# A hybrid backbone layer on one core: the later operands of seven products stored in two parts

## The chip, the core and the metric

The kernel runs on one core of a Trainium2 chip. The time is that of one execution on the device, in microseconds (us). The engines are TensorE (PE, matmuls; PEld is its weight loading), VectorE (DVE), ScalarE (ACT), GpSimd (POOL) and SyncE (SP, which here issues DMAs). All data are float32.

## What is computed

One layer for 1024 latent tokens and 256 context tokens of width 1024. A modulated, normalised input is projected by one wide matrix; then come windowed attention, a short gated convolution, a gated merge and an output projection, and a mixture of 16 experts. What matters here is the middle:

```
p = h @ w_in                        # columns: q, k, v | u, B, C | two gates
o = windowed attention of q, k, v   # 16 heads of 64, blocks of 128 queries
y = B * conv3(C * u)                # depthwise, width 3
merged = sigmoid(g_attn) * (o @ w_proj_attn) + sigmoid(g_conv) * (y @ w_proj_conv)
out = merged @ w_out
```

## The kernel before

TensorE multiplies float32 in parts: a number is stored as hi (its cast to the short format FR) and lo (what the cast left out, also as FR), and three matmuls, hi by hi, hi by lo and lo by hi, make a product. So an operand has to be split first: a ScalarE cast makes hi, a subtract on VectorE or GpSimd makes lo.

The program runs in stages. Attention (255 to about 597 us) goes through 32 units (class Unit), each of four heads by 128 queries; their matmuls and those of the two gate projections, 16 blocks of 48 (gate_half), stand between each other in an order that a scheduler made for ACT, DVE, PE and SP. What is left of the gate blocks is computed up to 624.9. At the end of a unit, ACT copies one half of its output from PSUM and DVE adds the other half; the result `ot`, 64 by 512, is stored to `od` in DRAM. On GpSimd a hand-written list of work (pool_work) runs beside it; its last items are o_sums(0) and o_sums(1), which load rows of `od` into tiles `acc` and `w` and make four sums of them.

The stage of the seven products (624.9 to 1054.6) computes the columns C, u, B of `p` and both projections. It is a loop over 20 pairs, each 128 columns of a weight and the same 128 columns 512 further on (class Pair). A pair is computed as a 2x2 block product in seven products instead of eight, one for each slot 0 to 6; a product is a call of block(), 12 matmuls of 128x512. The left operands are made from the weights (sums13, split22, sums24, split11, whose splits are the rows of L855 and L856). The right operands, four sums t1 to t4 and three plain blocks b11, b22, b21, are one set for pairs 0 to 11 (from the layer's input), a second set for pairs 12 to 15 (from `od`) and a third for pairs 16 to 19 (from the conv output `yd`). All three lie in the same SBUF buffers. In the order of slots 0 to 6 a pair takes t1, t3, b11, b22, t4, t2, b21. Normal pairs alternate between two groups of PSUM banks (names w, psT, psB, psF).

All engines run this stage in an order that is written by hand: the loop calls cur.product(slot), then the work of the slot, and then what at_turn(n, slot, f) has put there. For the second and third set, op_load(which, j) at turn (11 or 15, j + 1) loads the slot's operand, 1 MB, into its lo buffer, when the last pair of the old set has used it; op_split three turns later casts it to hi (L1005) and subtracts hi from it (L1006), half on DVE and half on POOL:

```
parts = ((nc.vector, slice(0, 2)), (nc.gpsimd, slice(2, 4)))
if which == 0 and j < 2:
    parts = ((nc.gpsimd, slice(0, 4)),)
```

The sums for t1 to t4 come from `sums[0]` and `sums[1]` in DRAM: of `od` by o_sums on POOL and, for the last two of four row blocks, by DVE in pairs 2 to 5 (o_late); of `yd` by DVE in pair 3m + 4 (sums_of). Weights come in by SP (L870), two tiles for each pair, one pair ahead.

Of the kernel before, what the change touches and what calls it, by code (L numbers as in the profile page):

```python
# [27 lines left out]
def hybrid_layer(ctx, tc, x, c, cx, c_ctx, w_mod, b_mod, norm1_g, w_in, attn_sink, conv_w,  # L28
# [60 lines left out]
    yd = dram.tile([NK, 128, T], F32, name="yd")  # L89
    sums = [dram.tile([4, NK // 2, 128, 512], F32, name=f"sums{i}") for i in range(2)]  # L90
# [370 lines left out]
    def mod_row(n, w_tile, acc_tile, more=False):  # L461


        def load(k):
            row, k = n + 2 + k // NK, k % NK
            w = w_tile()
            nc.gpsimd.dma_start(out=w, in_=w_mod[k * 128:(k + 1) * 128, row * 1024:row * 1024 + 1024])
            rws.append(w)

        if not rws:  # L470
            load(0)
            load(1)
            yield
        acc = acc_tile()
        for k in range(NK):
            w = rws.pop(0)
            nc.gpsimd.tensor_scalar(w if k else acc, w, sf[:, 0, k:k + 1], 1.0, op0=OP.mult, op1=OP.mult)
            if k:
                nc.gpsimd.tensor_tensor(out=acc, in0=w, in1=acc, op=OP.add)
            if k == NK - 1:  # L480
                nc.gpsimd.dma_start(out=rowp[n], in_=acc)
            if k < NK - 2 or more:
                load(k + 2)
            yield
# [122 lines left out]
    class Unit:  # L607
# [64 lines left out]
        def values(self, ci):  # L672
            if ci == 0:
                self.po = psB()
            th, tl = self.th.pop(ci)
            last = len(self.chunks) - 1
            nc.tensor.matmul(self.po, lhsT=self.v2t[:, self.chunks[ci]], rhs=th, start=(ci == 0), stop=False)
            nc.tensor.matmul(self.po, lhsT=self.v2t[:, self.chunks[ci]], rhs=tl, start=False, stop=(ci == last))  # L678
            if ci == last:
                g, i, po = self.g, self.i, self.po  # L680
                ot = at.tile([64, 512], F32, name="ot", bufs=3)
                nc.scalar.copy(out=ot, in_=po[64:128])
                nc.vector.tensor_tensor(out=ot, in0=po[0:64], in1=ot, op=OP.add)
                nc.sync.dma_start(out=od[g * 256:(g + 1) * 256, i * 128:(i + 1) * 128].rearrange("(h d) q -> d h q", h=4),
                                  in_=ot.rearrange("d (h q) -> d h q", h=4))
# [30 lines left out]
    def sums_of(eng, which, ks, p11, p12, p21, p22):  # L716

        for o_, a, b in ((p11, p12, p11), (p12, p22, p12), (p22, p22, p11), (p21, p21, p22)):
            eng.tensor_tensor(out=o_, in0=a, in1=b, op=OP.subtract)

    def sums_out(which, ks, p11, p12, p21, p22):
        for n, p in enumerate((p11, p12, p22, p21)):
            nc.sync.dma_start(out=sums[which][n, ks], in_=p)

    def o_rows(ks, p1, p2, eng=nc.sync):
        eng.dma_start(out=p1, in_=od[ks * 128:(ks + 1) * 128])
        for th in range(2):
            eng.dma_start(out=p2[th], in_=od[512 + ks * 128:512 + (ks + 1) * 128, th * 512:th * 512 + 512])
        return 0, ks, p1[:, 0:512], p1[:, 512:1024], *p2
# [7 lines left out]
    def pool_work():  # L737
        for n in range(1, 4):
            yield from mod_row(n, w_tile, lambda: osp.tile([128, 1024], F32, name="acc", bufs=2), n < 3)
        for ks in range(4):  # L740
            yield from x_sums(ks)
        for ks in range(2):

            yield from o_sums(ks)

    def o_sums(ks):
        o1, o2 = (osp.tile([128, 2, 512], F32, name=nm, bufs=2) for nm in ("acc", "w"))
        o = o_rows(ks, o1.rearrange("p a b -> p (a b)"), [o2[:, 0], o2[:, 1]], nc.gpsimd)
# [113 lines left out]
    class Pair:  # L862
# [39 lines left out]
        def quad(self, q):  # L902
# [33 lines left out]
            self.y_out(q)  # L936

        def y_out(self, q):
            if self.kind == 2 and q > 1:
                i = 3 - q  # L940
                nc.sync.dma_start(out=yd[self.m + 4 * i], in_=st["y"][i])
                if q == 3:
                    st["ys"] = (1, self.m, *[st["y"][a][:, b] for a in range(2) for b in (h0, h1)])
# [29 lines left out]
    def o_late(ks):  # L973
        st["o"] = o_rows(ks, mp_slot(7), [stage.tile([128, 512], F32, name="gs", bufs=2) for th in range(2)])
# [7 lines left out]
    def op_load(which, j):  # L982

        nm, at_ = takes[j]
        if nm[0] == "t":
            hi, lo = (tx.tile([128, 4, 512], FR, name=f"{nm}{hl}") for hl in range(2))
            src = sums[which][("t1", "t3", "t2", "t4").index(nm)].rearrange("k p f -> p k f")
        else:
# [3 lines left out]
            if which:  # L992
                src = yd[kh * 4:kh * 4 + 4, :, ts].rearrange("k p f -> p k f")
            else:
                src = od[kh * 512:kh * 512 + 512, ts].rearrange("(k p) f -> p k f", p=128)
        nc.sync.dma_start(out=lo.bitcast(F32), in_=src)
        opsets[which + 1][nm] = [hi, lo]

    def op_split(which, j):
        hi, lo = opsets[which + 1][takes[j][0]]  # L1000
        parts = ((nc.vector, slice(0, 2)), (nc.gpsimd, slice(2, 4)))
        if which == 0 and j < 2:
            parts = ((nc.gpsimd, slice(0, 4)),)
        for eng, ks in parts:
            nc.scalar.copy(out=hi[:, ks], in_=lo[:, ks].bitcast(F32))  # L1005
            eng.tensor_tensor(out=lo[:, ks], in0=lo[:, ks].bitcast(F32), in1=hi[:, ks].bitcast(F32), op=OP.subtract)  # L1006

    st, prev, later = {}, None, []

    def late_mults():  # L1010
        for q, o_, p in later:
            nc.gpsimd.tensor_tensor(out=o_, in0=p, in1=o_, op=OP.mult)
        prev.y_out(2)
        prev.y_out(3)
# [7 lines left out]
    for which, n in ((0, 12), (1, 16)):  # L1022
        for j in range(7):
            at_turn(n - 1, j + 1, lambda which=which, j=j: op_load(which, j))
            at_turn(n - 1, j + (5 if (which, j) == (0, 2) else 4), lambda which=which, j=j: op_split(which, j))
    for m in range(4):
        at_turn(3 * m + 4, 2, lambda: sums_of(nc.vector, *st["ys"]))
        at_turn(3 * m + 4, 5, lambda: sums_out(*st["ys"]))

    def row_load(n):  # L1030
        acc, small = mp_slot(4), mp_slot(5)
        br, nr = small[0:2, 0:512], small[0:2, 512:1024]
# [23 lines left out]
    for ks, b in ((2, 17), (3, 38)):  # L1056
        at_turn(0, b - 5, lambda ks=ks: o_late(ks))
        at_turn(0, b, lambda: sums_of(nc.vector, *st["o"]))
        at_turn(0, b + 3, lambda: sums_out(*st["o"]))
    at_turn(12, 5, late_mults)  # L1060
# [838 lines left out]
```

## Time and profile before

| | us |
|---|---|
| median of 3 runs | 1806.25 |
| lowest and highest | 1803.19 and 1810.12 |
| the profiled execution | 1805.46 |
| its span on the core | 1803.7 |

The profile is of one execution. Over the whole span TensorE is busy 1717.8 us (95%), VectorE 1418.4, ScalarE 1004.7 and GpSimd 553.5. The stage of the seven products takes 429.7 us of the span, attention about 342. Times of the trace are counted from the span's start. PEclk is the granted TensorE clock as a share of full speed; "idle before" is the time that an engine waited, and the arrow names what ended the wait.

### The profile page before, as it was taken

The page shows a single profiled execution, that of the slowest core. Times are in us where ns is not written, and L with a number is a line of the kernel's source. Part 1 is how long each engine was busy: PE and PEld are TensorE (multiplying, and loading weights), DVE is VectorE, ACT ScalarE, POOL GpSimd, SP SyncE. Part 2 cuts the span into 40 slices and gives each one's busy share as a digit, 9 for nine tenths or more (in the row PEclk, how much of TensorE's full clock was granted, in tenths as well). Part 3 has the DMA queues.
Part 4 walks back from the last instruction along what each step waited for, and adds up shares of the span by engine and source line. Part 5 has one row for each costly group of instructions (what it writes and reads, how often), then busy time and mean ns, then how long its engine had stood idle before and what let it go on. Part 6 is the DMA issues. An engine that isn't in the chain of part 4 may idle for free.

```text
span 1803.7 us, 24231 instructions
## 1 busy us (share of the span) xinstructions
PE 1717.8 (95%) x8421; PEld 1381.7 (77%) x8421; DVE 1418.4 (79%) x2018; ACT 1004.7 (56%) x1446; POOL 553.5 (31%) x408
## 2 busy tenths in 40 slices
PE   8999999999999999999797999949999999999997
PEld 5777887888877777778585877838788888888875
DVE  6857568877778357876978875579999999999996
ACT  6643157666767232232535333228778778878874
POOL 0034028778678100001535002240032223224001
PEclk8999999999999999999898999969999999999999
DMA  9465365555345723424556346688999999999855
GB/s 349 131 204 181 122 229 153 177 165 151 109 145 180 291 92 132 137 84 138 187 167 220 105 165 224 246 303 321 361 397 383 395 398 390 389 394 398 300 198 198
DMA packets 211654, 419.90 MB, mean 233 GB/s; under 512 B 17656, under 2 KB 107064, under 8 KB 209996
## 3 DMA queue, kind: packets, MB, share of 16 engines
q1 hardware_dynamic: 177356, 351.44, 53.7%
q0 software_dynamic: 12576, 46.47, 8.5%
q10 hardware_dynamic: 21600, 20.45, 3.2%
q8 instruction: 66, 1.08, 0.2%
q14 instruction: 56, 0.46, 0.1%
HBM read 345.41 MB, written 72.89 MB: 232 GB/s over the span
## 4 chain that ended last, share of the span: by engine, by line
PE 81%; DVE 7%; POOL 3%; issue 3%; DMA 3%; ACT 2%; SPq 0%; POOLq 0%; ACTq 0%; DVEq 0%
PE psA L1704 19%; PE w L843 9%; PE psT L843 5%; PE psB L1704 5%; PE psF L1704 5%; PE psA L1268 3%; PE psT L665 3%; PE psF L40 2%; PE psA L401 2%; PE psF L44 2%; PE psF L42 2%; PE psA L399 2%; PE psA L400 2%; PE psF L843 2%; PE psB L678 2%
## 5 line engine op out<-in xcount | busy, mean ns | idle before, releaser
L1704 PE MATMUL psA<-part,xeh 128*128 128x512 f32 x1024 | 282.0, 392 | 0.5 <-ACT xeh L1692 0.5
L1704 PEld LDWEIGHTS psA<-part,xeh 128*128 128x128 f32 x1024 | 191.5, 189 | 40.0 <-ACT xeh L1692 1.0
L1739 POOL DMA_INDIRECT md<-ye,idxs x15 | 107.9, 7191 | 213.2 <-DVE ye L1736 213.2
L1704 PE MATMUL psA<-part,xel 128*128 128x512 f32 x512 | 163.7, 391 | 0.0
L1562 DVE TENSOR_TENSOR part<-er,part 128x1024 fp32r<-128x1024 f32 x118 | 138.4, 1219 | 5.3 <-ACT part L1560 2.0
L1560 ACT CAST part<-er 128x1024 fp32r<-128x1024 f32 x118 | 123.7, 1056 | 33.2 <-PE psA L1704 19.9
L644 DVE CUSTOM_DVE_ANT_0 p<-psA,msk,nsink 128x640 f32<-128x640 f32 (+1 forms) x128 | 107.8, 843 | 27.4 <-PE psA L642 25.9
L669 DVE TENSOR_TENSOR tl<-psT,th 128x512 fp32r<-128x512 f32 x152 | 103.6, 686 | 23.7 <-ACT th L668 22.3
L660 POOL TENSOR_SCALAR p<-p,l 128x640 f32<-128x640 f32 (+1 forms) x128 | 101.0, 804 | 57.1 <-DVE l L658 16.0
L668 ACT CAST th<-psT 128x512 fp32r<-128x512 f32 x152 | 88.3, 585 | 49.0 <-PE psT L665 48.0
L648 ACT ACTIVATE p<-p,nm 128x640 f32<-128x640 f32 (+1 forms) x128 | 103.0, 805 | 21.3 <-DVE nm L644 20.6
L927 POOL TENSOR_TENSOR mp<-q,mp 128x512 f32<-128x512 f32 x15 | 24.3, 1648 | 290.8 <-DVE q L921 277.3
L1704 PEld LDWEIGHTS psA<-part,xel 128*128 128x128 f32 x512 | 96.3, 188 | 20.5 <-DVE xel L1693 0.3
L855 ACT CAST whi<-raw 128x1024 fp32r<-128x1024 f32 x40 | 42.0, 1049 | 121.6 <-DVE raw L886 85.3
L1562 DVE TENSOR_TENSOR part<-mh,part 128x1024 fp32r<-128x1024 f32 x88 | 105.1, 1220 | 5.1 <-ACT part L1560 2.4
L1562 DVE TENSOR_TENSOR part<-ml,part 128x1024 fp32r<-128x1024 f32 x88 | 105.4, 1219 | 4.6 <-ACT part L1560 1.6
L1560 ACT CAST part<-ml 128x1024 fp32r<-128x1024 f32 x88 | 92.3, 1053 | 25.9 <-PE psA L1704 17.5
L1562 DVE TENSOR_TENSOR part<-mp,part 128x1024 fp32r<-128x1024 f32 x85 | 100.8, 1220 | 6.9 <-ACT part L1560 4.3
L1560 ACT CAST part<-mh 128x1024 fp32r<-128x1024 f32 x88 | 92.2, 1053 | 25.1 <-PE psA L1704 16.5
L1560 ACT CAST part<-mp 128x1024 fp32r<-128x1024 f32 x88 | 92.0, 1053 | 24.9 <-PE psA L1704 16.4
L1704 PE MATMUL psB<-part,hhh 128*128 128x512 f32 x256 | 98.6, 396 | 0.2 <-ACT hhh L1692 0.2
L1704 PE MATMUL psF<-part,hhh 128*128 128x512 f32 x256 | 97.0, 390 | 0.0
(509 smaller groups left out, 4614.6 us busy)
## 6 DMA issues: line engine op xcount, KB each, us to landing
raw<-in_w_in_dram SPq DMA_DIRECT2D x49, 512.0 KB
er<-in_w_exp_down_dram SPq DMA_DIRECT2D x47, 512.0 KB
er<-in_w_exp_up_dram SPq DMA_DIRECT2D x38, 512.0 KB
mp<-in_w_exp_gate_dram SPq DMA_DIRECT2D x36, 512.0 KB
mh<-in_w_exp_up_dram SPq DMA_DIRECT2D x33, 512.0 KB
ml<-in_w_exp_up_dram SPq DMA_DIRECT2D x33, 512.0 KB
er<-in_w_exp_gate_dram SPq DMA_DIRECT2D x32, 512.0 KB
mh<-in_w_exp_gate_dram SPq DMA_DIRECT2D x29, 512.0 KB
```

The source lines that it names most:

```text
L644: nc.vector.tensor_tensor_reduce(out=p, in0=sp[:, 512 - n:768], in1=msk.rearrange("p a b -> p (a b)")[:, mo * 128:mo * 128 + n + L], op0=O ...
L648: nc.scalar.activation(out=p, in_=p, func=AF.Exp, scale=-1.0, bias=self.nm4[:, h:h + 1], accum_out=self.l4[:, h:h + 1])
L660: nc.gpsimd.tensor_scalar(self.pr[h], self.pr[h], l4[:, h:h + 1], 1.0, op0=OP.mult, op1=OP.mult)
L665: nc.tensor.transpose(pt[:, h * 128:(h + 1) * 128], self.pr[h][:, ci * 128:(ci + 1) * 128], ident)
L668: nc.scalar.copy(out=th, in_=pt)
L669: nc.vector.tensor_tensor(out=tl, in0=pt, in1=th.bitcast(F32), op=OP.subtract)
L843: nc.tensor.matmul(ps_, lhsT=w[a][:, o + k], rhs=xs[b][:, k], start=(first and k + a + b == 0), stop=(k == 3 and a == 1), skip_group_check ...
L1268: nc.tensor.matmul(pa[:, s], lhsT=a[t // 2][k // 4][:, k % 4, ts], rhs=w[k][:, s], start=(j == 0 and a is mh and w is woh), stop=(j == NK ...
L1560: nc.scalar.copy(out=hi, in_=raw)
L1562: eng.tensor_tensor(out=lo, in0=raw, in1=hi.bitcast(F32), op=OP.subtract)
L1704: nc.tensor.matmul(outs[s], lhsT=lh[:, k], rhs=wt[:, s * 512:s * 512 + 512], start=(k == 0 and n == 0), stop=(k == NK - 1 and n == 2))
L1739: nc.gpsimd.indirect_dma_start(out=md, out_offset=bass.IndirectOffsetOnAxis(ap=idxs[:, e:e + 1], axis=0), in_=ye, in_offset=None, compute_ ...
```

## The change

The operands of the second and third set are split where they are made, and DRAM holds their two parts.

- A unit of attention casts `ot` to `oh` on ACT and subtracts on DVE for `ol`, and stores all three: `od`, `odp[0]`, `odp[1]`. `ot` has two buffers instead of three.
- o_sums still makes the sums of the row blocks 0 and 1 on POOL; then parts_of casts them on ACT and subtracts on DVE, through the tiles `whi` and `wlo` that the gate blocks use, and sums_out stores both parts. `acc` has one buffer instead of two.
- The row blocks 2 and 3 are loaded, summed, split and stored at turns 0 to 18 (pairs 0 to 2), where before it was turns 12 to 41.
- y is split by y_split at pair 3m + 3 (slots 2, 3) and stored to `ydp`; its sums are made in slot 5 of that pair and split in the next.
- op_load loads hi and lo, 1 MB each; op_split is gone, and the multiplies that ran on POOL at pairs 10 and on run on DVE.

```
+                oh = at.tile([64, 512], FR, name="oh", bufs=2)
+                ol = at.tile([64, 512], FR, name="ol")
+                nc.scalar.copy(out=oh, in_=ot)
+                nc.vector.tensor_tensor(out=ol, in0=ot, in1=oh.bitcast(F32), op=OP.subtract)
+                for d, v in ((od, ot), (odp[0], oh.bitcast(F32)), (odp[1], ol.bitcast(F32))):
...
+    def parts_of(src, hi, lo):
+        nc.scalar.copy(out=hi, in_=src)
+        nc.vector.tensor_tensor(out=lo, in0=src, in1=hi.bitcast(F32), op=OP.subtract)
...
-        o1, o2 = (osp.tile([128, 2, 512], F32, name=nm, bufs=2) for nm in ("acc", "w"))
+        o1, o2 = osp.tile([128, 2, 512], F32, name="acc"), osp.tile([128, 2, 512], F32, name="w", bufs=2)
...
+        for i, o_ in enumerate((o1, o2)):
+            hi, lo = (stage.tile([128, 2, 512], FR, name=nm, bufs=2) for nm in ("whi", "wlo"))
+            parts_of(o_, hi, lo)
+            sums_out(0, ks, i, hi, lo)
...
-                if self.kind < 4 and self.n >= 10:
-                    nc.gpsimd.tensor_tensor(out=o_, in0=p, in1=o_, op=OP.mult)
...
-        nc.sync.dma_start(out=lo.bitcast(F32), in_=src)
+        for v, d in ((hi, src[0]), (lo, src[1])):
+            nc.sync.dma_start(out=v.bitcast(F32), in_=d)
...
-    def op_split(which, j):
...
-            at_turn(n - 1, j + (5 if (which, j) == (0, 2) else 4), lambda which=which, j=j: op_split(which, j))
...
-        at_turn(3 * m + 4, 2, lambda: sums_of(nc.vector, *st["ys"]))
+        n = 3 * m + 3
+        for i in range(2):
+            at_turn(n, 2 + i, lambda i=i: y_split(i))
+            at_turn(n, 3 + i, lambda i=i, m=m: y_out(i, m))
+        at_turn(n, 5, lambda: sums_of(nc.vector, *map(two, st["y"])))
+        for i in range(2):
+            at_turn(n + 1, 2 * i, lambda i=i: y_sums_split(i))
```

On SP the loads of the second set stand as follows in pair 11 and the first slots of pair 12; `raw` are the weights of pairs 12 and 13. Before:

```order
L870 DMA raw<-in_w_proj_attn_dram 128x8x128 x2
L996 DMA t_8193<-sums_79 128x4x512
L996 DMA t_8217<-sums_79 128x4x512
L996 DMA x_8237<-od 128x4x512
L996 DMA x_8260<-od 128x4x512
L996 DMA t_8279<-sums_79 128x4x512
L996 DMA t_8300<-sums_79 128x4x512
L870 DMA raw<-in_w_proj_attn_dram 128x8x128 x2
L996 DMA x_8340<-od 128x4x512
```

After the change:

```order
L888 DMA raw<-in_w_proj_attn_dram 128x8x128 x2
L1029 DMA t_8456<-sums_80 128x2048
L1029 DMA t_8457<-sums_80 128x2048
L1029 DMA t_8481<-sums_80 128x2048
L1029 DMA t_8482<-sums_80 128x2048
L1029 DMA x_8502<-odp 128x4x512
L1029 DMA x_8503<-odp 128x4x512
...
L888 DMA raw<-in_w_proj_attn_dram 128x8x128 x2
L1029 DMA x_8599<-odp 128x4x512
L1029 DMA x_8600<-odp 128x4x512
```

The order of the operands and the places of the weights are the same; each load has become two.

On ACT the end of attention is this before, from the `ot` of the third unit from the end (580.55 us) to the split of gate block 15 (the second row of L213; the first is block 14's); th are hi parts of a unit's attention weights, gs rows of a gate block that are done:

```order
L682 COPY ot<-psB 64x512
L668 CAST th<-psT 128x512 x3
L213 CAST whi<-raw 128x1024
L337 COPY gs<-psF 128x512
L668 CAST th<-psT 128x512 x2
L682 COPY ot<-psB 64x512
L668 CAST th<-psT 128x512 x4
L337 COPY gs<-psF 128x512
L682 COPY ot<-psB 64x512
L213 CAST whi<-raw 128x1024
```

After the change:

```order
L734 CAST whi<-w 128x1024
L688 COPY ot<-psB 64x512
L674 CAST th<-psT 128x512 x2
L692 CAST oh<-ot 64x512
L734 CAST whi<-acc 128x1024
L674 CAST th<-psT 128x512 x2
L339 COPY gs<-psF 128x512
L688 COPY ot<-psB 64x512
L734 CAST whi<-w 128x1024
L692 CAST oh<-ot 64x512
L215 CAST whi<-raw 128x1024 x2
```

Three of the four casts of the sums (L734) stand here between the rows of the last units, each unit has a cast of `oh` (L692), and the splits of the gate blocks 14 and 15 (L213, now L215 x2) come behind all of them, where block 14's stood ahead of the last two units' ot.

On POOL the pairs 10 to 12 have these rows before, behind the four sums of o_sums(1):

```order
L927 TENSOR_TENSOR mp_8035<-q,mp_8035 128x512
L927 TENSOR_TENSOR mp_8036<-q,mp_8036 128x512 x2
L1006 TENSOR_TENSOR t_8193<-t_8193,t_8192 128x2048
L1006 TENSOR_TENSOR t_8217<-t_8217,t_8216 128x2048
L1006 TENSOR_TENSOR x_8237<-x_8237,x_8236 128x1024
L1006 TENSOR_TENSOR x_8260<-x_8260,x_8259 128x1024
L1006 TENSOR_TENSOR t_8279<-t_8279,t_8278 128x1024
```

After the change POOL has nothing in the stage of the seven products: behind the same four sums (L731) comes work of a later stage.

```order
L731 TENSOR_TENSOR w<-w 128x512
L1414 MEMSET onesb 128x128
L1309 TENSOR_TENSOR r_9819<-ss_9818,nhalf 128x1 x2
L1316 TENSOR_TENSOR raw<-raw,whi 128x1024
L1317 DMA hd<-raw 128x1024
```

The subtracts of op_split and the multiplies of L927 have left the engine.

## Rows read from the trace of the kernel before

**Rows 1.** Busy time by stretch: pairs 11, 12, 15 and 16.

```profile
core 0: us, PE busy (x) PEld busy (x) DVE busy (x) ACT busy (x) POOL busy (x), PEclk, DMA share, GB/s
846.99:866.42 19.43, 19.43 (x86) 15.79 (x84) 16.91 (x15) 10.16 (x10) 7.47 (x4) 1.00 0.94 327
866.42:902.66 36.24, 25.80 (x85) 17.98 (x84) 33.37 (x22) 17.39 (x19) 23.22 (x8) 0.86 0.37 129
...
941.86:961.29 19.43, 19.43 (x85) 15.79 (x84) 13.95 (x14) 9.09 (x11) 7.40 (x5) 1.00 0.95 341
961.29:996.37 35.08, 25.94 (x86) 18.72 (x85) 31.70 (x22) 16.21 (x20) 22.98 (x9) 0.81 0.36 125
```

**Rows 2.** What ended TensorE's idle time before L843, 620 to 1060 us.

```profile
its engine sat idle before it (us, times) until:
  POOL t L1006: 6.0, 4
  DVE x L1006: 4.0, 1
```

**Rows 3.** Timeline of TensorE in pair 12: start, duration, instruction, idle before.

```profile
882.66 5.06 PE L843 MATMUL w<-x,x 128*128 128x512 f32 x11 [3.96 <-DVE x L1006]
```

**Rows 4.** Timeline of SyncE's queue: when DMAs are issued, and for how long.

```profile
845.82 3.49 SPq L870 DMA_DIRECT2D raw<-in_w_proj_attn_dram  x2
849.74 3.17 SPq L996 DMA_DIRECT2D t<-sums  x2
...
873.96 3.47 SPq L870 DMA_DIRECT2D raw<-in_w_proj_attn_dram  x2
877.52 0.54 SPq L996 DMA_DIRECT2D x<-od  x1
...
945.03 0.97 SPq L1066 DMA_DIRECT2D mp<-gd  x2
```

**Rows 5.** Bytes moved by DMA, 845 to 885 us, in 40 slices.

```profile
GB/s 0 13 234 272 5 197 341 367 358 281 223 399 401 408 383 401 385 383 365 389 391 391 383 293 72 29 0 0 0 0 195 318 11 168 335 414 365 291 0 0
```

**Rows 6.** Timelines of GpSimd and VectorE in pairs 11 and 12.

```profile
863.66 9.68 POOL L1006 TENSOR_TENSOR t<-t,t 128x2048 fp32r<-128x2048 f32 x2 [7.72 <-PE psB L843]
...
863.84 5.08 DVE L856 TENSOR_TENSOR x<-raw,x 128x512 fp32r<-128x512 f32 x1
...
869.44 4.45 DVE L885 TENSOR_TENSOR raw<-raw 128x512 f32<-128x512 f32 x1
873.93 0.69 DVE L886 TENSOR_TENSOR raw<-raw 128x512 f32<-128x512 f32 x1
...
876.95 1.22 DVE L856 TENSOR_TENSOR x<-raw,x 128x1024 fp32r<-128x1024 f32 x1
```

**Rows 7.** Busy time by stretch: attention (columns as in rows 1).

```profile
255.00:600.00 345.00, 334.44 (x1904) 280.18 (x1903) 267.65 (x533) 236.25 (x495) 261.60 (x251) 1.00 0.49 153
```

**Rows 8.** Attention: instructions on ot (ns min/median/max), and TensorE's longest wait (us, times, longest).

```profile
L682 ACT COPY ot<-psB x32: 582/584/589, 263.4 to 596.7; 64x512 f32<-64x512 f32 x32
L683 DVE TENSOR_TENSOR ot<-psB,ot x32: 652/682/684, 264.5 to 597.3; 64x512 f32<-64x512 f32 x32
...
PE psB L678 <- DVE tl L669: 6.8, 9, 1.2
```

**Rows 9.** Timelines of ScalarE and GpSimd at the end of attention.

```profile
558.13 1.05 ACT L711 CAST whi<-w 128x1024 fp32r<-128x1024 f32 x1 [2.79 <-POOL w L691]
...
562.00 1.06 ACT L711 CAST whi<-w 128x1024 fp32r<-128x1024 f32 x1 [1.11 <-DMA xd<-whi]
...
584.21 1.05 ACT L213 CAST whi<-raw 128x1024 fp32r<-128x1024 f32 x1
...
594.22 0.59 ACT L668 CAST th<-psT 128x512 fp32r<-128x512 f32 x1 [1.02 <-PE psT L665]
...
596.69 0.58 ACT L682 COPY ot<-psB 64x512 f32<-64x512 f32 x1
603.80 1.05 ACT L213 CAST whi<-raw 128x1024 fp32r<-128x1024 f32 x1 [6.53 <-PE psB L42]
...
582.23 0.57 POOL L726 DMA_DIRECT2D acc<-od  x1
...
586.89 1.29 POOL L719 TENSOR_TENSOR acc<-acc 128x512 f32<-128x512 f32 x1 [3.00 <-DMA acc<-od]
```

More of the change, by code (lines that the diff above doesn't have):

```diff
@@ L88, in hybrid_layer @@
     gd = dram.tile([2, NK, 128, T], F32, name="gd")
-    yd = dram.tile([NK, 128, T], F32, name="yd")
-    sums = [dram.tile([4, NK // 2, 128, 512], F32, name=f"sums{i}") for i in range(2)]
+    odp = dram.tile([2, H * HD, T], F32, name="odp")
+    ydp = dram.tile([2, NK, 128, T], F32, name="ydp")
+    sums = [dram.tile([4, 2, 128, 4, 512], F32, name=f"sums{i}") for i in range(2)]
     xd = dram.tile([4, 2, 128, 4, 512], F32, name="xd")
@@ L473, in mod_row @@
             yield
-        acc = acc_tile()
         for k in range(NK):
             w = rws.pop(0)
-            nc.gpsimd.tensor_scalar(w if k else acc, w, sf[:, 0, k:k + 1], 1.0, op0=OP.mult, op1=OP.mult)
+            nc.gpsimd.tensor_scalar(w, w, sf[:, 0, k:k + 1], 1.0, op0=OP.mult, op1=OP.mult)
             if k:
-                nc.gpsimd.tensor_tensor(out=acc, in0=w, in1=acc, op=OP.add)
+                if k == 1:
+                    acc = acc_tile()
+                nc.gpsimd.tensor_tensor(out=acc, in0=w, in1=first if k == 1 else acc, op=OP.add)
+            else:
+                first = w
             if k == NK - 1:
                 nc.gpsimd.dma_start(out=rowp[n], in_=acc)
-            if k < NK - 2 or more:
-                load(k + 2)
+            for i in {0: (), 1: (2, 3)}.get(k, (k + 2,)):
+                if i < NK or more:
+                    load(i)
             yield
@@ L935, in quad @@
             tt(out=o_, in0=p, in1=o_, op=OP.mult)
[L936 to L943, printed above, removed]
         def conv(self, i, part):
@@ L971, in signal, with two, o_load, o_split @@
             nc.scalar.activation(out=self.sig[q], in_=self.sig[q], func=AF.Sigmoid)
-    def o_late(ks):
-        st["o"] = o_rows(ks, mp_slot(7), [stage.tile([128, 512], F32, name="gs", bufs=2) for th in range(2)])
+    def two(t):
+        return t.rearrange("p (a b) -> p a b", a=2)
+    def o_load(ks):
+        st["o"] = ks, [two(mp_slot(7)), two(mp_slot(5))]
+        o_rows(nc.sync, ks, *st["o"][1])
+    def o_split(i):
+        o_ = st["o"][1][i]
+        st["op"] = two(mp_slot(6)).bitcast(FR), o_.bitcast(FR)
+        parts_of(o_, *st["op"])
+    def y_split(i):
+        src = st["y"][i]
+        if i == 0:
+            src, both = src[:, h0], mp_slot(7).bitcast(FR)
+            st["yp"] = both[:, h0], both[:, h1]
+        else:
+            st["yp"] = [mp_slot(j).bitcast(FR) for j in (6, 5)]
+        parts_of(src, *st["yp"])
+    def y_out(i, m):
+        for hl, v in enumerate(st["yp"]):
+            nc.sync.dma_start(out=ydp[hl, m + 4 * i, :, 0:v.shape[-1]], in_=v.bitcast(F32))
+    def y_sums_split(i):
+        y = two(st["y"][i])
+        st["yp"] = two(mp_slot(6 + i)).bitcast(FR), y.bitcast(FR)
+        parts_of(y, *st["yp"])
     takes = (("t1", (tx, "t1")), ("t3", (tx, "t3")), ("b11", (0, 0)), ("b22", (1, 1)), ("t4", (tx, "t4")), ("t2", (tx, "t2")), ("b21", (1, 0)))
@@ L986, in op_load @@
             hi, lo = (tx.tile([128, 4, 512], FR, name=f"{nm}{hl}") for hl in range(2))
-            src = sums[which][("t1", "t3", "t2", "t4").index(nm)].rearrange("k p f -> p k f")
+            src = [sums[which][("t1", "t3", "t4", "t2").index(nm), hl] for hl in range(2)]
         else:
@@ L992, in op_load @@
             if which:
-                src = yd[kh * 4:kh * 4 + 4, :, ts].rearrange("k p f -> p k f")
+                src = [ydp[hl, kh * 4:kh * 4 + 4, :, ts].rearrange("k p f -> p k f") for hl in range(2)]
             else:
-                src = od[kh * 512:kh * 512 + 512, ts].rearrange("(k p) f -> p k f", p=128)
-        nc.sync.dma_start(out=lo.bitcast(F32), in_=src)
+                src = [odp[hl, kh * 512:kh * 512 + 512, ts].rearrange("(k p) f -> p k f", p=128) for hl in range(2)]
+        for v, d in ((hi, src[0]), (lo, src[1])):
+            nc.sync.dma_start(out=v.bitcast(F32), in_=d)
         opsets[which + 1][nm] = [hi, lo]
-    def op_split(which, j):
[L1000 to L1014, printed above, removed]
+    st, prev = {}, None
     mps = [None] * NK
@@ L1055, in hybrid_layer @@
         at_turn(2 * n + 2, 5, row_out)
[L1056 to L1060, printed above, removed]
+    for ks, b in ((2, 0), (3, 10)):
+        at_turn(0, b, lambda ks=ks: o_load(ks))
+        at_turn(0, b + 3, lambda: sums_of(nc.vector, *st["o"][1]))
+        for i in range(2):
+            at_turn(0, b + 4 + 3 * i, lambda i=i: o_split(i))
+            at_turn(0, b + 5 + 3 * i, lambda i=i: sums_out(0, st["o"][0], i, *st["op"]))
     def gate_rows(p):
```

43 lines of the change are left out of this document (18 added, 25 removed).

## The prediction

> **What bounds the kernel now.** I read three views in this order: the windows, to find where TensorE works at less than its pace; then the waits and the timelines of the engines around those places; then the DMA's bytes per microsecond. In the stage of the seven products a pair takes 19.43 us, with TensorE busy all of it at full clock; two pairs do not keep that pace. Pair 12, the first that uses operands made from the attention output, takes 36.24 us, and pair 16, the first on the conv output, 35.08 us [rows 1]. They lose 16.81 and 15.65 us, 32.46 together: the most that the change can win in this stage. TensorE is idle for 10.44 and 9.14 us of that (window less busy); the rest is its clock, 0.86 and 0.81 in the mean. Who ends the idle time is the split that the change deletes: GpSimd's subtract 6.0 us, VectorE's 4.0 us for one operand [rows 2]. [...]
>
> Why the splits are late has two causes, and the change takes away one. The bytes come late: a slot's buffers are free for reloading only when pair 11 has used them, so the first load is issued at 849.74 and the last, b21, at 877.52 behind pair 13's weights [rows 4]. And GpSimd's subtracts run long and hold VectorE: while GpSimd needed 9.68 us for two of them, a VectorE subtract that takes 0.69 us took 5.08, and another 4.45 [rows 6].
>
> [...]
>
> **The change part by part: loads instead of splits (A).** Splits no longer stand between landing and matmul; but each operand now comes as two loads of 1.05 MB. Fourteen are 14.68 MB, where seven were 7.34. They follow the same buffers as before, so they can't start earlier: the loads' bytes begin near 851.9 (bytes move in 846 to 849 and again from 850, the slices of the two weight tiles issued at 845.82; 0.52 MB each) [rows 4, 5]. From then on a slot frees 2 MB every 2.8 us, more than the queue carries, so the DMA is always full. When it was, the twelve 1-us slices 856 to 867 average 390 GB/s [rows 5]. 14.68 MB at 390 is 37.6 us, and pair 13's weights, 1.05 MB in small pieces at the 234 and 272 GB/s of their slices, 4.1 us: b21 has landed at 893.6. Its product is due six slots of 2.78 us after 866.42, at 883.1. Pair 12 loses 10.5 us, plus one restart at half clock, 2.5: 13.0 us. The other operands are less late (t4 by about 1 us, t2 by about 3), so they add nothing. Pair 16 is alike, and two gate rows of 0.52 MB are ahead of its second load [rows 4], 2.7 us: 15.7. Together 28.7 against 32.46: **-3.8 us**. Bounds: at the best of those slices, 408 GB/s, and with no loss of clock, 8.9 and 11.5, which is -12.1; at 341 GB/s, the mean of the window of pair 15 where the DMA was busy 95% [rows 1], b21 lands 5.4 us later, 18.4 and 21.5, which is +7.4. I take 390, since it is the rate of these very operands in full slices.
>
> [...]
>
> **Attention makes the parts (B).** Each of 32 units gets a ScalarE cast and a VectorE subtract of 64x512, and two stores of 128 KB more, 8.4 MB in a stage whose DMA is half idle, at 153 GB/s [rows 7]. The nearest rows are the copy and the add on the same tile: 0.584 and 0.682 us [rows 8], so 18.7 us for ScalarE and 21.8 for VectorE in a stage of 345 us, where TensorE is busy 334.4, VectorE 267.7, ScalarE 236.3 and GpSimd 261.6 [rows 7]. TensorE bounds it and hides them unless an instruction queued behind them is one that TensorE waits for. There is such: it waits nine times for VectorE's tl, 6.8 us in all, 0.76 each [rows 8]. The subtract stands ahead of a later tl in VectorE's fixed order. If a cast is late, everything behind its subtract is late too. Below: nothing. Above: a wait of 0.76 in one unit of three, 11 times, 8.3 us. I take three more waits, **+2 us**, since the mean loads of 84% and 74% that result leave gaps.
>
> **The end of attention (C).** The sums of the first two row blocks are split there: four casts and subtracts through two pairs of buffers, one of which gate block 13 holds until 603.80, when block 15's cast can have it [rows 9]. So the four steps and block 14's split pass one after the other through the other pair, each cast waiting for the store before it: the same chain before took 3.87 us from cast to cast, 558.13 to 562.00 [rows 9]. And the accumulator has one buffer now, so GpSimd's second load waits for the first subtract. With the first cast near 584, its subtract near 586.5, the second load and sums 4.7 + 5.4 us later (582.23 to 586.89, and four of 1.29) [rows 9], the third cast stands at 596.6, the fourth at 600.5, block 14's at 604.4, ready near 606; before the change it stood at 584.21 [rows 9]. ScalarE runs in order, and the third cast is queued ahead of the last unit's last th and ot, which came at 594.22 and 596.69 [rows 9]. So the end of attention is pushed by some 2.4 (596.6 less 594.22) to 3.9 us (one more step), and block 14 then by nothing. I take **+4 us**; below 0, if TensorE has enough gate matmuls in its order to cover it, above two steps and a late tile, 9.
>
> **The stage's VectorE (D).** The early pairs have room: pairs 0 to 10 need no split. Pairs 3, 6, 9 and 12 take a split of y, 0.69 + 1.22 us, and the four sums from their successors, 4 x 0.69 [rows 6], 4.7 us on pairs with about 13.9 of 19.43 busy: 18.6, close to full. **+1 us**, from 0 to 3 (0.7 for each of four). The multiplies that come back from GpSimd to VectorE at pairs 10 and on cost 0.7 us each, in pairs that lose the halves of the splits.
>
> The sum: 1805.46 - 3.8 + 2 + 4 + 1 = **1808.7**. The profiled execution lies 0.8 below the median of the three runs, 1806.25, so I keep it as it is.
>
> **The rivals.** One: the loads don't bind (faster). Then the best rate holds, the clock is not lost, and the releases from GpSimd's hold show: A is -12.1, and with the attention's cost half hidden (B + C + D = +3) the time is 1796.4. For it: the splits are what ends TensorE's idle time [rows 2], and VectorE's 5.08 us goes [rows 6]. Against: the loads' slices are full already where half the bytes moved [rows 5]. It decides if b21 lands before 892.
>
> Two: the cost moves to where the parts are made (slower). The last units' chain of casts and stores runs at two steps more than I take, and tl is late in one unit of three: B 8.3, C 9, D 1, A -3.8, that is 1820. For it: one serial chain, and orders that hold other work behind it. Against: TensorE's idle time there is only 10.6 of 345 us. It decides if the stage from 255 to 624.9 grows by more than 10 us.
>
> Three: the loads run at the 341 GB/s of pair 15's window, and the boundaries are longer than before, although their splits are gone: 1805.46 + 7.4 + 7 = 1819.9. Against: in that window the DMA had 5% idle, and pieces of 512 bytes in it. [...]
>
> **How the numbers follow.** The forecast has 0.52; rival one 0.22; rival two 0.18; rival three 0.08. The bounds of the forecast's own terms reach from 1797 to 1816; to leave out 2 in 10, the range goes from 1796 to 1820. 0.5%, about what a measurement of this kernel tells from no change, is 9 us: faster is below 1797.2, slower above 1815.3. Faster has rival one's 0.22; slower has two and three and a bit of the forecast, 0.27; within 0.51.
>
> **What would show it.** Right: no split in the stage; pair 12 near 32.4 and pair 16 near 35 us, the idle time in them ended by DMA for t2 and b21, 1-us slices at 380 to 400 GB/s from 852 to 893; first matmul of pair 0 some 4 to 8 us after 624.9; pairs 0 to 11 as before, within 1 us. Wrong: pair 12 below 28 us (loads faster or earlier than I think), a stage of attention longer by over 10 us, or stops inside pairs 3, 6 and 9.

## The result, and the profile after

The changed kernel takes 1826.9 us in the median (4 runs, 1822.94 to 1827.92), against 1806.26 before in the same comparison: 1.13% slower, ratio 1.0113 with a 95% interval of 1.0099 to 1.0128. The profiled execution took 1827.22 us, with a span of 1825.3, 21.6 more than before. The forecast was 1808.7 us, with a range of 1796 to 1820: the measured time lies above it, on the side of rival two.

Where the 21.6 us lie, by the first matmul of each pair (the profiled executions of both):

| stretch | before | after | difference | forecast |
|---|---|---|---|---|
| attention up to the 31st ot | 589.43 | 602.71 | +13.3 | B: +2 |
| to the first matmul of pair 0 | 624.94 | 646.09 | +7.9 more | C: +4 |
| pairs 0 to 11 | 241.5 | 246.5 | +5.0 | D: +1 |
| pairs 12 to 16 | 129.95 | 126.96 | -3.0 | A: -3.8 |
| from pair 17 to the end | 807.3 | 805.7 | -1.6 | 0 |

The windows of the pairs that the change is made for, 12 and 16, come out as worked out: 32.48 and 35.54 us against the 32.4 and 35 of the forecast (columns as in [rows 1]).

```profile
892.60:925.08 32.48, 24.57 (x85) 18.04 (x84) 16.96 (x23) 9.62 (x12) 0.00 (x0) 0.86 1.04 391
984.02:1019.56 35.54, 25.51 (x86) 18.15 (x85) 13.76 (x18) 6.54 (x9) 0.00 (x0) 0.86 0.94 348
665.52:689.00 23.48, 21.49 (x85) 16.77 (x84) 15.90 (x21) 7.43 (x10) 0.00 (x0) 0.93 0.61 202
```

POOL does nothing there now, DVE half of what it did, and the DMA is full through pair 12 (1.04, 391 GB/s). The third row is pair 1, 19.43 us long before: the clearest loss of the pairs 0 to 11. TensorE's idle time before the products, which the splits ended in [rows 2], is now ended by loads, 17.9 us in 12 stops:

```profile
  DMA x<-ydp: 7.6, 5
  DMA t<-sums: 6.3, 4
  DMA x<-odp: 4.0, 3
```

Up to the 31st ot, TensorE runs 1853 matmuls in both kernels. Before and after (columns as in [rows 1]):

```profile
255.00:589.43 334.43, 324.07 (x1853) 271.92 (x1852) 263.59 (x527) 232.15 (x488) 258.89 (x249) 0.99 0.48 151
255.00:602.71 347.71, 330.26 (x1853) 273.40 (x1852) 293.74 (x557) 248.76 (x521) 266.11 (x245) 0.99 0.57 165
```

Of the 13.3 us, 7.1 are idle time (17.45 against 10.36) and 6.2 are more busy time for the same number of matmuls, part of it at a lower clock: the granted clock is 0.50 in 371 to 373 and in 575 to 578, behind the two longest stops. TensorE's longest waits in attention and at its end (us, times, longest; in [rows 8] tl is 6.8, 9, 1.2):

```profile
PE psB L684 <- DVE tl L675: 9.0, 7, 2.7
PE psB L683 <- ACT th L674: 4.2, 2, 3.9
PE psB L683 <- DVE ot L689: 3.4, 2, 3.1
```

The stops for tl became longer, not more frequent, and others joined them (the 3.9 for th is at the end, shown further down). The longest stop for tl is at 368.49. The timelines of DVE, POOL and PE around it, then all 32 of that instruction (ns, min/median/max):

```profile
362.74 5.10 DVE L693 TENSOR_TENSOR ol<-ot,oh 64x512 fp32r<-64x512 f32 x1
367.77 0.67 DVE L675 TENSOR_TENSOR tl<-psT,th 128x512 fp32r<-128x512 f32 x1
...
363.08 3.13 POOL L666 TENSOR_SCALAR p<-p,l 128x640 f32<-128x640 f32 x4
366.19 1.11 POOL L478 TENSOR_SCALAR w<-w,sf 128x1024 f32<-128x1024 f32 x1
...
368.49 0.50 PE L684 MATMUL psB<-tl,v2t 128*128 128x512 f32 x1 [2.66 <-DVE tl L675]
...
L693 DVE TENSOR_TENSOR ol<-ot,oh x32: 674/1050/5098, 266.5 to 617.4; 64x512 fp32r<-64x512 f32 x32
```

The new subtract starts at 362.74, just before GpSimd begins five instructions in a row, and ends 0.5 us after the last of them: 5.10 us instead of 0.67. Everything behind it on DVE is late, and TensorE stops for the next tl. The 32 subtracts took 38.5 us, 1.2 each.

The longest stop up to the 31st ot has another cause. ScalarE and TensorE there:

```profile
570.04 1.04 ACT L722 CAST whi<-w 128x1024 fp32r<-128x1024 f32 x1 [3.46 <-POOL w L702]
573.19 0.47 PE L683 MATMUL psB<-th,v2t 128*128 128x512 f32 x1 [3.06 <-DVE ot L689]
```

A cast of GpSimd's x sums (sums of the layer's input, made by pool_work) waits for GpSimd, the copy of a unit's ot stands behind it on ScalarE, and TensorE waits 3.06 us. The same stop is in two of the kernels below, with attention's parts alone (3.07 us) and without the part stores (3.04).

The end of attention, ScalarE, then GpSimd and TensorE:

```profile
597.46 1.05 ACT L734 CAST whi<-acc 128x1024 fp32r<-128x1024 f32 x1
...
601.30 1.05 ACT L734 CAST whi<-w 128x1024 fp32r<-128x1024 f32 x1 [0.34 <-DMA sums<-whi]
...
610.48 1.04 ACT L734 CAST whi<-acc 128x1024 fp32r<-128x1024 f32 x1 [5.10 <-DMA sums<-whi]
611.43 1.07 ACT L674 CAST th<-psT 128x512 fp32r<-128x512 f32 x2
...
600.06 0.59 POOL L744 DMA_DIRECT2D acc<-od  x1 [3.70 <-DVE wlo L735]
606.13 1.36 POOL L731 TENSOR_TENSOR acc<-acc 128x512 f32<-128x512 f32 x1 [4.94 <-DMA acc<-od]
...
612.06 0.52 PE L683 MATMUL psB<-th,v2t 128*128 128x512 f32 x1 [3.92 <-ACT th L674]
```

The chain is the one described: the first subtract frees acc, GpSimd loads and sums (4.94 us for the load), the third cast follows, and the last unit's last two th stand behind it. From the first cast to the third are 13.0 us, 12.6 in the forecast. TensorE stands for 3.92 us, and the clock is 0.57 in 612 to 616.

### The profile page after: what moved, and what is told of

Same layout as the page of the kernel before. It is cut to its first block, busy times and chain, and to the rows that moved or that the text cites. A ratio compares the mean times of both kernels' runs of the same rounds, so it can differ in the third digit from the quotient of the medians.

```text
span 1825.3 us, 24427 instructions
## 1 busy us (share of the span) xinstructions
PE 1724.7 (94%) x8420; PEld 1383.9 (76%) x8421; DVE 1431.6 (78%) x2080; ACT 1016.4 (56%) x1476; POOL 491.6 (27%) x374
## 4 chain that ended last, share of the span: by engine, by line
PE 77%; DVE 8%; DMA 6%; issue 3%; POOL 3%; ACT 2%; SPq 1%; ACTq 0%; POOLq 0%; DVEq 0%
PE psA L1728 19%; PE w L861 8%; PE psT L861 6%; PE psB L1728 5%; PE psF L1728 5%; PE psA L1292 3%; PE psF L861 3%; PE psT L671 2%; PE psA L403 2%; PE psA L401 2%; PE psA L402 2%; PE psF L40 2%; PE psF L44 2%; PE psF L42 2%; DMA t<-sums 2%
## 5 line engine op out<-in xcount | busy, mean ns | idle before, releaser
L666 POOL TENSOR_SCALAR p<-p,l 128x640 f32<-128x640 f32 (+1 forms) x128 | 107.7, 857 | 61.9 <-DVE l L664 25.5
L671 PE MATMUL psT<-identr,p 128*128 128x128 f32 x608 | 94.5, 275 | 2.9 <-POOL p L666 2.5
```

Source lines behind the costliest of these rows:

```text
L666: nc.gpsimd.tensor_scalar(self.pr[h], self.pr[h], l4[:, h:h + 1], 1.0, op0=OP.mult, op1=OP.mult)
L671: nc.tensor.transpose(pt[:, h * 128:(h + 1) * 128], self.pr[h][:, ci * 128:(ci + 1) * 128], ident)
```

## The experiments

Every kernel was compared with the kernel before on the same chip; the median of before was 1804.2 to 1806.2 us. "Pair 0" is its first matmul in the profiled execution, 624.9 before and 646.1 after the change; "unit 26" is the ot of the 26th unit, 9.4 us later after the change. Only one execution of each kernel is profiled, and attention varies between them: in the change and in the kernel with the row blocks later (below), whose code up to pair 0 is the same, unit 26 lies 3.7 us apart and pair 0 6.5. A smaller difference between two kernels is not shown by their profiles alone.

**Attention's parts alone.** The kernel before, with the unit's edit of the change and its single acc buffer:

```
+ oh = at.tile([64, 512], FR, name="oh", bufs=2)
+ ol = at.tile([64, 512], FR, name="ol")
+ nc.scalar.copy(out=oh, in_=ot)
+ nc.vector.tensor_tensor(out=ol, in0=ot, in1=oh.bitcast(F32), op=OP.subtract)
+ for d, v in ((od, ot), (odp[0], oh), (odp[1], ol)): nc.sync.dma_start(...)
```

> The kernel before, in which only each unit of attention also casts oh, subtracts ol and stores both (nobody reads them), with the single acc buffer of the change. Theory, GpSimd's hold on VectorE in ol: ol has a mean of 1.0 us or more instead of 0.68 and maxima of several us, the units run 8 to 13 us late by the end, and the time is 1814 to 1819 us. Rival, only the chain of casts and stores at the end of attention costs (it is not in this kernel): 1806 to 1809 us.

Measured: 1818.47 us against 1804.93 (ratio 1.0076, 1.0059 to 1.0093), pair 0 at 639.6, unit 26 10.2 us late. So B by itself is 14.7 us at pair 0 and 13.5 in time, not 2. The stop for tl is there again, at 367.34.

**The same, ol from PSUM.**

```
- nc.vector.tensor_tensor(out=ol, in0=ot, in1=oh.bitcast(F32), op=OP.subtract)
+ nc.vector.tensor_tensor(out=ol, in0=po[0:64], in1=oh.bitcast(F32), op=OP.subtract)
```

> As the kernel with attention's parts alone, but the subtract for ol reads half of the output from PSUM instead of the finished sum from SBUF (same size; ol then holds other numbers, which nobody reads). Theory, the hold: a subtract with one SBUF input isn't held, ol falls to 0.68 to 0.75 us at most 1, and the time to 1807 to 1811 us. Rival, it is the number of instructions and stores, not their length: as the kernel with attention's parts, within 2 us.

The 32 subtracts, here and in the kernel above it (ns, min/median/max):

```profile
L692 DVE TENSOR_TENSOR ol<-psB,oh x32: 673/678/683, 266.9 to 607.8; 64x512 fp32r<-64x512 f32 x32
```

```profile
L692 DVE TENSOR_TENSOR ol<-ot,oh x32: 676/1075/5110, 265.4 to 614.4; 64x512 fp32r<-64x512 f32 x32
```

With one SBUF input none of the 32 is held (0.683 us at most, 5.110 with two), and unit 26 is 1.6 us late instead of 10.2. But the time is 1815.63 (ratio 1.0067, 1.0045 to 1.0088), above the 1807 to 1811 that I expected and not apart from the kernel above by the intervals, and pair 0 comes at 633.9: in the last units other stops appear, among them 4.6 us for gs, which ScalarE makes behind a cast that waits for GpSimd's x sums:

```profile
562.50 0.79 PE L40 MATMUL psF<-x,whi 128*128 128x512 f32 x1 [4.64 <-ACT gs L338]
```

The edit moves some rows in the scheduler's orders too, so the two kernels differ by more than the one operand.

**The same without the subtract.** oh is cast and stored twice; ol is gone.

> The kernel with attention's parts alone, without the subtract for ol: oh is cast and stored twice in its place, so ScalarE's casts and all 64 stores stay. Theory, VectorE's subtract is what makes attention late (its own length and GpSimd's hold on it): unit 26 within 3 us of before, pair 0 at 625 to 631, time 1805 to 1811 us. Rival, casts and stores cost by themselves: pair 0 at 635 or later, 1814 us or more.

1812.03 us against 1806.05 (1.0031, 1.0019 to 1.0044), pair 0 at 632.9: between theory and rival. Unit 26 is 0.6 us late, as the theory has it; the loss comes at 571 to 578 in one stop. VectorE and TensorE there:

```profile
576.11 1.23 DVE L215 TENSOR_TENSOR wlo<-raw,whi 128x1024 fp32r<-128x1024 f32 x1 [5.33 <-DMA xd<-wlo]
```

```profile
577.99 0.79 PE L683 MATMUL psB<-tl,v2t 128*128 128x512 f32 x1 [4.76 <-DVE tl L674]
```

A gate block's split waits for the buffer wlo, which a store of GpSimd's x sums has not left: it was issued at 567.75 and landed by 576.1, 8.3 us later, where the same split began 3.8 us after that store's issue before the change (565.13 to 568.92). Two tl queue behind the split. The DMA was busy 96% in 564 to 568, with two stores of oh just ahead of this one, and GpSimd's loads for o_sums, issued from 566.57 on, are ahead of it too, where before the change they came behind it (565.72). Which of these made it land late was not tried.

**The same without the stores.** `for d, v in ((od, ot),):` in place of the three.

> The kernel with attention's parts alone, in which oh and ol are made but not stored: the 64 stores and their 37 us of issue on SyncE are gone. Theory, as above: it stays near the kernel with attention's parts, unit 26 about 10 us late, time 1814 to 1819 us. Rival, SyncE's queue and the DMA make attention late: 1809 us or less.

1816.09 us (1.0051, 1.0033 to 1.0070), pair 0 at 634.6, unit 26 7.7 us late, ol up to 5.1 us: as the theory has it, most of the lateness stays. Pair 0 is 5.0 us earlier than with the stores and unit 26 2.4, less than two executions of the same code differ, and the intervals of the times overlap. So that the stores cost time by themselves is not shown.

**The loads alone.** The kernel before with each later operand loaded twice from the unsplit rows, no op_split, and the multiplies on VectorE.

```
- nc.sync.dma_start(out=lo.bitcast(F32), in_=src)
+ for v in (hi, lo): nc.sync.dma_start(out=v.bitcast(F32), in_=src)
- at_turn(n - 1, ..., lambda which=which, j=j: op_split(which, j))
```

> The kernel before with the loads of the change alone: each operand of the second and third set is loaded twice, 1 MB for hi and 1 MB for lo, from the unsplit rows, and nothing is split (the later products so have other numbers). It is term A alone. As forecast: pair 12 near 32.4 us and pair 16 near 35, time 1801 to 1804 us. Rival, the loads don't bind and the gain was eaten elsewhere: pair 12 below 28, time 1794 or less.

1804.72 us against 1804.93 (0.9996, 0.9986 to 1.0006): no gain at all, neither theory nor rival. Pair 12 takes 34.83 and pair 16 36.82 us, 71.65 together, against 71.32 before and 68.02 with the change. That is 3.6 us worse than the same bytes in the changed kernel, and the bytes per microsecond show why. First this kernel from 847 to 902, then the changed one from 873 to 923, in 40 slices each:

```profile
GB/s 253 106 185 290 255 259 276 405 408 378 386 392 383 389 387 389 384 387 387 389 386 386 387 384 390 386 384 380 362 346 314 408 404 314 198 408 420 429 383 272
```

```profile
GB/s 228 191 63 323 348 328 275 347 393 426 413 419 398 403 390 390 390 385 387 385 390 419 421 419 419 419 419 426 419 364 340 332 305 413 405 395 397 354 303 420
```

Reading the old layout, in 2 KB per row block and partition, runs mostly at 383 to 392. The change also lays the sums out in DRAM so that a partition's 8 KB lie together, which the list of the change does not say: the slices of its t run at 413 to 426, and those of b11 and b22, which kept the old pieces, at 385 to 390. Eight of the fourteen loads are sums; at 420 in place of 387 their 8.4 MB take an estimated 1.7 us less, 3.4 for both boundaries. In both kernels the first slices of these loads are not full: 255 to 290 from 851 to 856 here, 275 to 348 from 877 to 883 there.

**The change without attention's parts.** Unit as before; b11, b22 and b21 loaded twice from od.

> The changed kernel without oh and ol in attention: b11, b22 and b21 are loaded twice from the unsplit rows instead (so these products have other numbers). Everything else as changed. Theory, attention's parts cost 9 to 13 us and the chain at its end 5 to 8: the time falls to 1813 to 1818 us. Rival, the chain at the end makes nearly all of it: 1823 or more. A second rival, the chain only hurts because attention is late: 1808 or less.

1823.66 us (1.0113, 1.0091 to 1.0135; single runs from 1818.0 to 1828.5, the profile is of the fastest): the first rival's figure, not the theory's. Up to the 31st ot attention is 1.6 us late, and the last ot then 7.0: the chain at the end costs this even if attention is on time. But pair 0 comes at 640.1, with a stop of 5.4 us for its weights: their load is issued at 631.69, behind gate stores for which SyncE waited 7.5 us, so what follows the chain isn't C as the change has it. In time this kernel is 18.7 us over before and the change 20.6, with the intervals over each other: attention's parts cost 13.5 us alone, but taking them out of the change gives back 1.9 by the medians. The two costs do not add up.

**The change without the chain.** The sums of row blocks 0 and 1 are stored whole and split in the pairs.

```
- parts_of(o_, hi, lo); sums_out(0, ks, i, hi, lo)        # at the end of attention
+ nc.sync.dma_start(out=osd[ks, i], in_=o_)
+ for ks, b in ((2, 0), (3, 7), (0, 14), (1, 32)): ...    # load, split, store in the pairs
```

> The changed kernel without splits at the end of attention: the sums of row blocks 0 and 1 are stored whole and split in the pairs 2 and 4 to 5, the row blocks 2 and 3 in pairs 0 and 1. Theory, the chain of casts and stores costs what the last unit loses (5.4 us) and what follows to pair 0 (2.5 us): pair 0 starts near 639, as in the kernel with attention's parts alone, and the time is 1817 to 1821 us. Rival, attention is late anyway and the chain hid in that: 1825 or more.

1815.01 us against 1804.18 (1.0057, 1.0040 to 1.0074): 10.8 over before, where the change is 20.6 over it, and pair 0 at 638.9, as expected. C is 7.2 us at pair 0; the time falls by 9.8, a little more than expected, and the intervals are apart.

**ol from PSUM in the changed kernel,** and **both edits.** The unit's sum is finished in PSUM; ot, oh and ol are made from there.

```
- nc.vector.tensor_tensor(out=ot, in0=po[0:64], in1=ot, op=OP.add)
+ nc.vector.tensor_tensor(out=po[0:64], in0=po[0:64], in1=ot, op=OP.add)
+ nc.scalar.copy(out=ot, in_=po[0:64])
```

> The changed kernel, in which a unit's sum is finished in PSUM, so that the subtract for ol has one SBUF input; the price is one more ScalarE copy of 0.58 us in each unit. Theory, GpSimd's hold on VectorE: ol falls from 1.2 to 0.7 us, unit 26 comes 5 to 8 us earlier, time 1818 to 1823 us. Rival, attention suffers from the number of instructions in the orders: 1826 us or more, with ScalarE's copies on top.

> The two edits together: no splits at the end of attention, and ol from PSUM. If both causes are what they seem, their gains add up: 1810 to 1815 us. If one hides in the other, as the better of the two within 2 us.

ol falls to 0.68 us each, but the times are 1828.01 (1.0134, 1.0117 to 1.0151) and, with the chain gone too, 1816.55 (1.0070, 1.0053 to 1.0087): nothing is won in time, though pair 0 of the second comes 4.5 us earlier than without the PSUM edit. The first is where its rival put it (1826 or more), and the two edits together are not better than the better of the two (1815.01). Both have a stop of 4.7 us for tl near 578, of the kind shown above. In these kernels a copy of 0.58 us was added, so they can't tell how much of it is its price.

**The row blocks 2 and 3 later.** `for ks, b in ((2, 12), (3, 32)):` in place of `((2, 0), (3, 10))`.

> The changed kernel with its sums of the row blocks 2 and 3 at turns 12 to 20 and 32 to 40 instead of 0 to 18. Theory, pair 1's loss of 4.05 us comes from VectorE's sums and splits standing ahead of the weights' split there: pair 1 returns to 19.4 us and at most 2 us come back in pairs 2 and 5, time 1822 to 1825 us. Rival, it comes from the weights landing late, since all loads behind attention's end are late: pair 1 stays above 21 us, 1826 us or more.

Pairs 1 and 6 of that kernel (columns as in [rows 1]):

```profile
672.00:691.44 19.44, 19.44 (x86) 15.79 (x84) 11.05 (x15) 5.52 (x8) 0.00 (x0) 1.00 0.33 109
774.52:800.14 25.62, 23.55 (x90) 16.97 (x88) 20.95 (x28) 6.20 (x8) 0.00 (x0) 0.93 0.46 157
```

Pair 1 is whole again, though its weights land as late as in the change (VectorE waits 6.65 us for them, 6.49 there). So the loss there is VectorE's work ahead of the weights' split. But it turns up in pair 6, 25.62 instead of 21.37, where the moved sums and splits stand ahead of the weights in the same way and TensorE waits 1.34 and 0.72 us. The time is 1829.10 (1.0125, 1.0108 to 1.0142), not the 1822 to 1825 of the theory and not apart from the change. Attention, whose code is the same, was 3 to 4 us slower in this execution.

**A mixed kernel: only the sums in parts.** Attention and its end as before; t1 to t4 in parts, made in the pairs; b11, b22 and b21 loaded whole and split on ScalarE and VectorE.

```
+ def op_split(which, j):
+     hi, lo = opsets[which + 1][takes[j][0]]
+     for ks in (slice(0, 2), slice(2, 4)):
+         parts_of(lo[:, ks].bitcast(F32), hi[:, ks], lo[:, ks])
+ for j, t in ((2, 0), (3, 1), (6, 5)):
+     at_turn(n, t, lambda which=which, j=j: op_split(which, j))
```

> A mixed kernel: attention and its end as before; only the four sums t1 to t4 are stored and loaded in parts (split in the pairs 0 to 5 and in 3m + 4), while b11, b22 and b21 are loaded whole and split by ScalarE and VectorE, without GpSimd. 11 loads instead of 14: at 390 GB/s b21 lands near 885.6 of the old time and is split by 888. Theory: pair 0 near 625, pair 12 near 27 us, pair 16 near 30, time 1789 to 1796 us. Rival, VectorE's work in the pairs 0 to 5 and the splits' place cost as much: 1800 us or more.

1792.22 us against 1804.18 (0.9929, 0.9913 to 0.9946), in the theory's range. Pair 0 at 624.3, pair 12 25.09 us, pair 16 30.99.

**The same, with b21 first.** b21 is loaded ahead of the next weights and split in slot 1; the last gate rows are loaded four turns earlier.

```
- at_turn(n - 1, j + 1, lambda which=which, j=j: op_load(which, j))
+ at_turn(n - 1, min(j + 1, 6), lambda which=which, j=j: op_load(which, j))
- for j, t in ((2, 0), (3, 1), (6, 5)):
+ for j, t in ((2, 0), (3, 1), (6, 1)):
```

> The mixed kernel with sums in parts, in which b21 is loaded ahead of the next pair's weights and split in slot 1 of its pair, and the last two gate rows are loaded four turns earlier. Theory, the boundaries are bound by the bytes ahead of b21: the weights (4.1 us) and the gate rows (2.7 us) leave that queue, pair 12 falls to 21 to 23 us, pair 16 to 23 to 26, the time to 1779 to 1787 us. Rival, VectorE waits at the early split and holds the next pair's sums: pair 13 or 17 grows by what 12 and 16 win, 1790 us or more.

1784.94 us against 1806.17 (0.9890, 0.9872 to 0.9909): the fastest kernel here, 42 us under the change. Its pairs 12, 13 and 16:

```profile
865.99:889.11 23.12, 20.01 (x85) 15.63 (x84) 17.02 (x20) 11.38 (x13) 0.00 (x0) 1.00 1.03 376
889.11:912.47 23.36, 20.25 (x85) 15.54 (x84) 19.64 (x27) 11.15 (x14) 0.00 (x0) 1.00 0.63 188
951.34:975.54 24.20, 21.51 (x86) 16.79 (x84) 18.10 (x22) 11.08 (x14) 0.00 (x0) 0.93 0.79 297
```

The clock stays full through pair 12 (1.00, 0.86 in [rows 1]). Little of the rival is true: pair 13 takes 23.36 where the kernel before takes 19.76, but the mixed kernel without this edit already took 22.45. In both, VectorE's sums of its weights stand behind b21's split, which here waits 3.68 us for the cast.

## Why the prediction was wrong

**A was right in its sum, -3.8 against -3.0, in part by luck.** The forecast of pairs 12 and 16 met 32.48 and 35.54 us, and loads ended the stops. But the rate was not one rate: the sums came at 413 to 426 GB/s, through a layout that I had not priced, and the blocks at 385 to 390. At the rate that I took, as in the kernel with the loads alone, TensorE's last stop of pair 12 ends 30.5 us after the pair's start instead of my 27.2 (27.6 in the changed kernel), and A is nothing: pairs 12 to 16 take 129.97 us there, 129.95 before. The ends of that stop, with the loads alone and with the change (their pairs 12 start at 866.32 and 892.60):

```profile
896.78 4.53 PE L843 MATMUL w<-x,x 128*128 128x512 f32 x11 [3.19 <-DMA x<-od]
920.22 5.06 PE L861 MATMUL w<-x,x 128*128 128x512 f32 x11 [2.14 <-DMA x<-odp]
```

One thing that I had wrong is "the DMA is always full" from 851.9 on: the first 5 us move 255 to 290 GB/s. The faster sums, with 419 in seven slices of the changed kernel, made up for what was missing. The 2.5 us for "one restart at half clock" are an estimate from [rows 3]: eleven matmuls took 5.06 us there, at a granted clock of 0.50 (882.66 to 887.72), and would take 2.5 at the 0.23 us of a pair's 84 in 19.43. No run shows them as the loss of a boundary: after the change TensorE is busy 24.57 us in pair 12 and 25.51 in pair 16, at a clock of 0.86, 5.1 and 6.1 more than 19.43, and idle 7.9 and 10.0, where A counts 10.5 and 13.2.

**B is the step that failed: "the nearest rows are the copy and the add on the same tile ... 0.682", and with it "three more waits" of 0.76.** The add has a PSUM input; the new subtract has two in SBUF. Under [rows 6] I told how GpSimd holds such a subtract, 5.08 us instead of 0.69, and counted its going only as a gain in the products. Attention, where GpSimd is busy 261.6 of 345 us [rows 7], was where that row had its price: 1.2 us in the mean, stops up to 2.7 us for the tl behind. B was 13.3 us, above its bound of 8.3. That the hold makes the units late up to unit 26 is shown: 10.2 us with it, 1.6 with one PSUM input, 0.6 without the subtract. That the subtract costs time is shown too: without it 1812.03 instead of 1818.47, with the intervals apart. It is not the whole of B. The forecast counted only waits for tl, and those grew by 2.2 us (9.0 against 6.8); the rest is, for the most part, the stop of 3.06 us behind the cast of the x sums and 6.2 us more busy time. And without the subtract, casts and stores (with the single acc buffer) still cost 8.0 us at pair 0 and 6.0 us of time, most of it in one stop near 578, where a store of the x sums lands late and holds the buffer of a split. When one stop is taken away, another follows: from the kernel with attention's parts to that with ol from PSUM pair 0 gains 5.7 us and the time 2.8, inside its interval. Taken out of the change, attention's parts gave back only 1.9 us of time. How much of B each cause would have alone stays open, because each edit also moves the scheduler's orders.

**C had the right chain and too small an end.** Its links fit (13.0 us against 12.6 from first cast to third), and removing it gave 7.2 us at pair 0 and 9.8 of time. The lateness of the last unit was 5.4 us instead of 2.4 to 3.9. The step that failed is that I set the third cast's start against the last th (594.22). In the order after the change two th stand behind that cast, and the cast itself takes 1.04 us. The first of the two stood here before:

```profile
592.61 0.59 ACT L668 CAST th<-psT 128x512 fp32r<-128x512 f32 x1 [1.01 <-PE psT L665]
```

With attention's 13.3 us that is 605.9, and it came at 611.43, 5.5 later. I also left out the clock behind the stop of 3.92 us, 0.57 in 612 to 616, and "block 14 then by nothing" was wrong: after the last ot 2.5 us more are lost, among them 1.39 us in which TensorE waits for ot and 0.92 for block 14's wlo.

**D was 5.0 instead of +1, and not where I put it.** The split of y cost nothing that shows in pairs 6 and 9, which have it: they take 21.37 and 19.43 us, and took 21.86 and 19.43 before. (The even pairs 2 to 8 were above 19.43 before the change too, which "two pairs do not keep that pace" passes over; no sum rests on it.) Pair 3 lost 1.4 us, but in a stop ahead of its split of y. VectorE and TensorE there:

```profile
707.75 1.22 DVE L735 TENSOR_TENSOR mp<-mp,mp 128x1024 fp32r<-128x1024 f32 x1
717.60 2.58 PE L861 MATMUL psF<-x,x 128*128 128x512 f32 x10 [0.73 <-DVE x L874]
726.24 1.82 DVE L735 TENSOR_TENSOR mp<-mp,mp 128x512 fp32r<-128x512 f32 x2
```

The first row is the last split of row block 3, ahead of the weights' rows; the third is y's. The mixed kernels, which split such a row block there and no y, lose 1.3 us in pair 3 as well. That split alone was not tried. The rest, 4.05, is pair 1, which I had called roomy: pairs 0 to 2 take the sums and splits of row blocks 2 and 3, 5.2 us each, and I counted those as hidden. There the next weights land late, and sums and splits then stand ahead of their split. VectorE, ScalarE and TensorE in pair 1:

```profile
660.92 0.69 DVE L894 TENSOR_TENSOR raw<-raw 128x512 f32<-128x512 f32 x1 [6.49 <-DMA raw<-in_w_in_dram]
```

```profile
670.51 1.05 ACT L873 CAST whi<-raw 128x1024 fp32r<-128x1024 f32 x1 [4.14 <-DVE raw L904]
```

```profile
672.55 0.73 PE L861 MATMUL psF<-x,x 128*128 128x512 f32 x2 [1.27 <-ACT x L873]
```

**The rivals and the range.** Rival two came in, with a chance of 0.18; its condition, 255 to 624.9 longer by over 10 us, was met by 21. The place was right and its price of 1820 too low, but its two mechanisms are not what the traces show: the chain ran as I took it up to the third cast, not two steps longer, and the stops for tl were fewer (7 against 9) and longer, not one in three units. The bounds of my four terms, added up, reach from 1793 to 1833 us; the 1797 to 1816 that I gave for them, and the range from it, do not follow from them as written.

## What to carry to other kernels

Before work is moved to another stage, price it in the conditions of that stage: which engines run beside it, what their rows there show of each other, and what stands behind it in their orders. A row that shows a hold has to be applied on both sides of a change, to what is removed and to what is added. And where a transfer is the limit, halving what is doubled (parts only for the sums, which pairs can make, whole loads with a split for the rest) can win what the full idea loses: 1784.94 us here against 1826.9.

## What the hardware showed that I had not expected

A VectorE subtract of 64x512 with two SBUF inputs took from 0.67 to 5.10 us beside GpSimd's work in attention, and 0.67 to 0.68 in all 32 cases when one of the two lay in PSUM. Loads in pieces of 8 KB moved 413 to 426 GB/s, in pieces of 2 KB mostly 383 to 392, both with the DMA full (a busy share of 1.04 and 1.05 in pair 12).
